# The output projection of a hybrid decoder layer, by one level of Strassen's scheme

## The chip, the cores and the metric

The kernel runs on one core of one Trainium2 chip. The metric is the device time of one execution in microseconds (us); a kernel is run several times and the median counts. TensorE (PE) multiplies matrices, VectorE (DVE), ScalarE (ACT) and GpSimd (POOL) do the element-wise work, SyncE (SP) mostly issues DMAs. A matmul's stationary operand is loaded first (PEld), its moving operand of 512 columns then streams through, and the sums stay in one of eight PSUM banks of 128x512 float32. The working memory is SBUF, with 128 partitions.

## The reference, cut to what matters

```python
h = rmsnorm(x, pre_g)                                # x: (1024, 1024) float32
z = h @ w_in                                         # one input projection, split into the parts below
a_out = chunked_sgu(gelu(a_u), gelu(a_v), ...) * silu(a_gate)    # branch A: (1024, 1024)
b_out = rmsnorm_per_head(gla_chunked(q, k, v, log_a)) * silu(b_gate)   # branch B: (1024, 1024)
mixed = concatenate([a_out, b_out], -1)              # (1024, 2048)
y = mixed @ w_out                                    # w_out: (2048, 1024)
return x + rmsnorm(y, post_g)
```

Only the last two lines are touched: a product of 1024 x 2048 by 2048 x 1024, a norm over each row of the result, and the residual.

## The kernel before

Every large product is done in three matmuls per pair of tiles (mm3, L105 to L109). A float32 operand is split into a rounded part "hi" and the rest "lo", both of the type float32r: ACT casts hi (L102), DVE subtracts it from the source to get lo (L103), and TensorE adds hi*hi + hi*lo + lo*hi into a PSUM bank. A split of a 128x512 tile is thus one ACT and one DVE instruction; the DVE one reads two operands from SBUF.

The order of work is: the norm of x and its transposed, split form hT (four tiles of tag "q" in pool hp); branch B head by head, whose features end up in four tiles mixB (feature-major, 128 features x 1024 tokens at a time); branch A, whose features end up in place in the tiles vn (read through mixed_a: 128 features x 512 tokens); the output projection. In branch A the last steps are, for the eighth group of channels, a projection out of hT, an ACT activation into u (L587) and a DVE product into vn (L592).

The output projection takes the tokens in two halves. For a half it goes through the 16 feature tiles in four groups of four. For each feature tile it loads the 128 rows of w_out (L620, 512 KB, into three slots "raw" of the pool wts), splits both halves of the columns into granules wh and wl (nine slots each) and splits the feature tile into mm. The B features come first, since the A features are the last to be ready. Eight banks hold the sums of four token tiles by two column halves; every group adds 96 matmuls, so there are 2 x 4 x 96 = 768. In the last group of a half each token tile is finished in turn: ACT squares and sums a bank (L653), DVE multiplies it by post_g (L660), DVE and POOL make the reciprocal root (L95, L98), DVE scales and adds the residual (L662), and SP and ACT issue the stores.

Tiles come from pools; tiles of one tag share a number of slots, and a pool that is opened where another was closed takes over its bytes. The kernel states no order by hand. A planner simulates the program when it is built: of the instructions that are ready in its simulated time it puts the one that comes first in the program on the engine's queue, gives out slots, and derives all waits. On the chip each queue then runs in that fixed order. Loads, casts and subtractions of a later tile can so be queued ahead of the work of an earlier one, as far as slots are free. That is how the first w_out loads come to stand in SP's queue some 70 us before the projection begins: the slots "raw" and the granules are those of the input projections before it, and the first two mm tiles have a place of their own in vnp (the later ones take over the bytes of hT).

Of the kernel before, what the change touches and what calls it, by code (L numbers as in the profile page):

```python
# [8 lines left out]
F32 = mybir.dt.float32  # L9
F32R = mybir.dt.float32r  # L10
# [5 lines left out]
P = 128  # L16
# [17 lines left out]
def hybrid_layer(  # L34
# [28 lines left out]
    hp = ctx.enter_context(tc.tile_pool(name="hp", bufs=1))  # L63
# [41 lines left out]
    def mm3(ps, a, b, start, stop):  # L105
        """ps += a^T b, with a and b given as their two parts"""
        nc.tensor.matmul(ps, a[0], b[0], start=start, stop=False)  # L107
        nc.tensor.matmul(ps, a[0], b[1], start=False, stop=False)  # L108
        nc.tensor.matmul(ps, a[1], b[0], start=False, stop=stop)  # L109

    W = 512
    # the pre norm's gain goes into the rows of w_in: one column of it for each k tile
    gain = const.tile([P, KT], F32, name="gain")

    def split_scaled(hi, lo, src, k):
        """the two parts of src times the gain of k tile k"""
        g = gain[:, k : k + 1]
        nc.scalar.activation(out=hi, in_=src, func=AF.Copy, scale=g)  # L118
        nc.vector.scalar_tensor_tensor(  # L119
            out=lo, in0=src, scalar=g, in1=hi.bitcast(F32), op0=ALU.mult, op1=ALU.subtract  # L120
        )
# [10 lines left out]
    def block_a(cols, before=lambda k2: None):  # L132
        """512 columns of w_in, k tile by k tile: [(hi, lo)] of [P, 512]"""
        got = []
        for k2 in range(KT // 2):
            before(k2)
            raw = wts.tile([P, 2, W], F32, tag="raw", name="raw", bufs=3)
# [12 lines left out]
    def block_b(cols):  # L150
        """two times 128 columns of w_in: [(hi, lo)] by k of [P, 256]"""
        got = []
        for k4 in range(KT // 4):
            raw = wts.tile([P, 4, 256], F32, tag="raw", name="raw", bufs=3)
# [19 lines left out]
    def proj_tok(ts, blk):  # L174
        """[tok, col] = h[tok tile] @ w, for the token tiles ts"""
# [8 lines left out]
    def proj_col(hf, blk, i):  # L184
        """[col, tok] = (h @ w)^T for the 128 columns i of a block and a half of the tokens"""
# [8 lines left out]
    # v and gate of the first head, and the low-rank weights, wait in slots of the mixed features  # L194
# [15 lines left out]
    with tc.tile_pool(name="pre", bufs=2) as pre:  # L210
# [48 lines left out]
        for t in range(NT - 2):  # L259
# [6 lines left out]
            if t == 3:  # L266
                # columns by groups of 32: hi, hi, lo, hi
# [13 lines left out]
    mixB = []  # L281
    with tc.tile_pool(name="gla", bufs=1) as gp:
# [12 lines left out]
        # low-rank weights by groups of 32 rows, to meet lr's parts: hi, lo, hi, hi  # L295
# [14 lines left out]
        # lr by groups of 32 rows: h w_hi twice rounded, h w_lo, and what the rounding left  # L310
# [20 lines left out]
        def gates(hd, hf):  # L331
            """exp of b - b_ref, b_ref - b, b_last - b and b, feature-major"""
# [6 lines left out]
            # 16 * log_a = min(z, 0) - ln(1 + exp(-|z|))  # L339
# [38 lines left out]
        def qk(hd, got):  # L378
            """q and k of a head, with their decays, in tiles of two chunks"""
# [42 lines left out]
        def attend(hd, t, got, v, sg, cur):  # L422
            """output of one tile of two chunks, and the state after it"""
# [179 lines left out]
    def mixed(n, hf):  # L603
        """tile n of the mixed features (B first) for a half of the tokens: [P, 4, P]"""
        if n < 8:
            return mixB[n // 2][:, n % 2, hf * 512 : (hf + 1) * 512].rearrange("p (t c) -> p t c", c=P)
        return mixed_a(n - 8, hf)

# [1 line left out]
    with tc.tile_pool(name="outp", bufs=2) as op:  # L610
        pog = op.tile([P, D], F32, name="pog", bufs=1)
        nc.gpsimd.dma_start(pog, row_bc(post_g, D))
        for hf in range(2):
            acc = []
            for n4 in range(0, 16, 4):
                ws, ms = [], []
                for n in range(n4, n4 + 4):
                    e = (n + 8) % 16
                    raw = wts.tile([P, 2, W], F32, tag="raw", name="raw", bufs=3)
                    nc.sync.dma_start(  # L620
                        raw.rearrange("p a b -> p (a b)"), w_out[e * P : (e + 1) * P, :]
                    )
                    ws.append(weight_granules(2, [P, W]))
                    for j in range(2):
                        split(*ws[-1][j], raw[:, j])
                    i = 16 * hf + n
                    if i == 0:
                        mm = vnp.tile([P, 2, 2, 4, P], F32R, tag="wg", name="mm")
                    elif i % 4 == 2:
                        mm = hp.tile([P, 2, 4, 4, P], F32R, tag="q", name="mm", bufs=4)  # L630
                    i = (i - 2) % 4 if i >= 2 else i
                    ms.append((mm[:, 0, i], mm[:, 1, i]))
                    split(*ms[-1], mixed(n, hf))
                for t in range(4):
                    if n4 == 0:
                        acc.append([bank(), bank()])
                    last = n4 == 12
                    order = [(i, j) for i in range(4) for j in range(2)]
                    if last:
                        order.sort(key=lambda o: o[1])  # L640
# [50 lines left out]
```

## Time and profile before

| | before |
|---|---|
| median of 3 runs | 807.33 us (806.49 to 807.36) |
| profiled execution, span from first to last instruction | 805.6 us |
| what lies around the span in the runs | 0.9 to 1.8 us |
| PE busy | 787.2 us (98%) |
| DVE, ACT, POOL busy | 49%, 42%, 16% |
| output projection, first to last matmul | 624.8 to 799.0 us |

The profile gives one execution with the start and length of every instruction, and what ended each wait. Of the profiled execution the page gives the span alone; its own time stands beside the other runs in the second and third line. Matmuls overlap each other in the records (each shows 389 ns, while a new one starts every 0.227 us), so a sum of durations overstates PE; its pace is read from start times.

### The profile page before, as it was taken

To read this page: it belongs to the slowest core of one execution; us is meant where nothing else is said; L and a number is where in the kernel's file an instruction comes from. 1 tells how busy PE (TensorE), PEld (TensorE's weight loads), DVE (VectorE), ACT (ScalarE), POOL (GpSimd) and SP (SyncE) were. 2 spreads that over 40 slices of the span, in tenths; PEclk is the share of its full clock that TensorE was granted. 3 is DMA by queue.
4 is the path that set the end of the run, shared out by engine and by line. 5 is a ranking of instruction groups with operands and counts; after the bars stand their busy time and mean duration, and the time that the engine had idled before them with its cause. 6 is when DMAs were issued, how large, how long until landed. Compare 5 with 4: busy or idle time off the path is not lost.

```text
span 805.6 us, 10163 instructions
## 1 busy us (share of the span) xinstructions
PE 787.2 (98%) x3865; PEld 656.8 (82%) x3865; DVE 392.8 (49%) x736; ACT 336.8 (42%) x678; POOL 126.7 (16%) x161
## 2 busy tenths in 40 slices
PE   5999999999999999999999999999999999999996
PEld 4888888887888788888888888888888888888885
DVE  4536688337633763342424996233332613663235
ACT  6628567336633763241414315343432512542222
POOL 2341243221222122120001350000000000010001
PEclk9999999999999999999999999999999999999999
DMA  9303101003100310031503011111110333473304
GB/s 285 116 8 111 52 1 54 1 1 111 54 1 1 111 53 1 1 105 52 157 1 105 0 53 53 52 53 53 53 53 8 125 104 104 145 264 115 105 27 156
DMA packets 48913, 58.53 MB, mean 73 GB/s; under 512 B 3864, under 2 KB 38688, under 8 KB 48864
## 3 DMA queue, kind: packets, MB, share of 16 engines
q1 hardware_dynamic: 45488, 49.36, 20.0%
q0 software_dynamic: 2224, 7.47, 3.0%
q10 hardware_dynamic: 1152, 1.05, 0.4%
q8 instruction: 30, 0.49, 0.3%
q14 instruction: 19, 0.16, 0.1%
HBM read 53.68 MB, written 4.19 MB: 72 GB/s over the span
## 4 chain that ended last, share of the span: by engine, by line
PE 93%; ACT 3%; DVE 2%; DMA 1%; issue 1%; POOL 0%; SPq 0%; POOLq 0%; DVEq 0%; ACTq 0%
PE ps L107 29%; PE ps L108 29%; PE ps L109 29%; PE ps L571 2%; PE ps L318 1%; PE ps L464 1%; DMA raw<-in_w_in_dram 1%; PE ps L238 1%; PE ps L413 1%; ACT wh L118 0%; ACT L349 0%; PE ps L403 0%; PE ps L405 0%; ACT L348 0%; DVE b L352 0%
## 5 line engine op out<-in xcount | busy, mean ns | idle before, releaser
L107 PE MATMUL ps<-wh,hT 128*128 128x512 f32 x384 | 152.0, 397 | 2.3 <-ACT hT L102 2.3
L107 PE MATMUL ps<-hT,wh 128*128 128x512 f32 x384 | 150.7, 393 | 0.0
L109 PE MATMUL ps<-wh,hT 128*128 128x512 f32 x384 | 150.7, 393 | 0.0
L108 PE MATMUL ps<-wl,hT 128*128 128x512 f32 x384 | 150.3, 392 | 0.0
L109 PE MATMUL ps<-hT,wl 128*128 128x512 f32 x384 | 149.8, 390 | 0.0
L108 PE MATMUL ps<-hT,wh 128*128 128x512 f32 x384 | 149.6, 390 | 0.0
L108 PE MATMUL ps<-wl,mm 128*128 128x512 f32 x256 | 99.3, 389 | 0.0
L109 PE MATMUL ps<-wh,mm 128*128 128x512 f32 x256 | 99.3, 389 | 0.0
L107 PE MATMUL ps<-wh,mm 128*128 128x512 f32 x256 | 96.2, 389 | 0.0
L119 DVE SCALAR_TENSOR_TENSOR wl<-raw,gain,wh 128x256 fp32r<-128x256 f32 (+1 forms) x144 | 87.1, 654 | 18.2 <-ACT wh L118 18.0
L118 ACT ACTIVATE wh<-raw,gain 128x256 fp32r<-128x256 f32 (+1 forms) x144 | 74.1, 573 | 30.6 <-PE ps L108 14.8
L107 PEld LDWEIGHTS ps<-wh,hT 128*128 128x128 f32 x384 | 72.7, 189 | 17.0 <-ACT hT L102 2.7
L109 PEld LDWEIGHTS ps<-wh,hT 128*128 128x128 f32 x384 | 72.5, 189 | 14.9 <-DVE hT L103 0.5
L109 PEld LDWEIGHTS ps<-hT,wl 128*128 128x128 f32 x384 | 72.1, 188 | 15.0
L103 DVE TENSOR_TENSOR wl<-raw,wh 128x512 fp32r<-128x512 f32 x64 | 42.9, 690 | 84.5 <-ACT wh L102 84.5
L108 PEld LDWEIGHTS ps<-wl,hT 128*128 128x128 f32 x384 | 72.7, 189 | 13.9
L108 PEld LDWEIGHTS ps<-hT,wh 128*128 128x128 f32 x384 | 72.2, 188 | 14.6
L107 PEld LDWEIGHTS ps<-hT,wh 128*128 128x128 f32 x384 | 72.2, 188 | 14.2
L102 ACT CAST wh<-raw 128x512 fp32r<-128x512 f32 x64 | 38.7, 622 | 98.8 <-PE ps L109 74.4
L108 PEld LDWEIGHTS ps<-wl,mm 128*128 128x128 f32 x256 | 48.1, 188 | 10.1
L109 PEld LDWEIGHTS ps<-wh,mm 128*128 128x128 f32 x256 | 48.1, 188 | 9.9
L107 PEld LDWEIGHTS ps<-wh,mm 128*128 128x128 f32 x256 | 48.0, 188 | 9.9
(166 smaller groups left out, 927.8 us busy)
## 6 DMA issues: line engine op xcount, KB each, us to landing
raw<-in_w_in_dram SPq DMA_DIRECT2D x80, 256.0 KB, 3.6
raw<-in_w_out_dram SPq DMA_DIRECT2D x32, 512.0 KB, 4.1
raw<-in_w_in_dram SPq DMA_DIRECT2D x8, 512.0 KB, 3.9
xr<-in_x_dram POOLq DMA_DIRECT2D x8, 512.0 KB, 4.4
xt<-in_x_dram SPq DMA_DIRECT2D x7, 512.0 KB, 5.5
out_dram<-yo SPq DMA_DIRECT2D x8, 256.0 KB, 2.1
out_dram<-yo ACTq DMA_DIRECT2D x8, 128.0 KB, 2.1
out_dram<-yo SPq DMA_DIRECT2D x8, 128.0 KB, 2.4
```

What stands on the lines that cost most here:

```text
L102: nc.scalar.copy(out=hi, in_=src)
L103: (eng or nc.vector).tensor_tensor(out=lo, in0=src, in1=hi.bitcast(F32), op=ALU.subtract)
L107: nc.tensor.matmul(ps, a[0], b[0], start=start, stop=False)
L108: nc.tensor.matmul(ps, a[0], b[1], start=False, stop=False)
L109: nc.tensor.matmul(ps, a[1], b[0], start=False, stop=stop)
L118: nc.scalar.activation(out=hi, in_=src, func=AF.Copy, scale=g)
L119: nc.vector.scalar_tensor_tensor(out=lo, in0=src, scalar=g, in1=hi.bitcast(F32), op0=ALU.mult, op1=ALU.subtract)
L238: nc.tensor.transpose(pt[:, k * P : (k + 1) * P], h[:, kk * P : (kk + 1) * P], ident)
L318: nc.tensor.matmul(pl, w_lr[:, k], part, start=(k == 0 and i == 0), stop=(k == KT - 1 and i == 1),)
L413: nc.tensor.transpose(pt[:, j * P : (j + 1) * P], ks[:, 2 * j : 2 * j + 2].rearrange("p n c -> p (n c)"), ident,)
L464: nc.tensor.transpose(ptv[:, k, i], og[:, i, k * P : (k + 1) * P], ident)
L571: nc.tensor.matmul(pt[:, c], part[:, c], wsT[:, g], start=True, stop=True)
```

## The change

The product is cut into blocks: rows of the result into the two token halves, the 2048 features into B (index 1) and A (index 2), the columns of w_out into two halves. Instead of eight block products there are seven, by the form of Strassen's scheme in which sums are reused: with S1 = A21 + A22, S2 = S1 - A11, S3 = A22 - S2 (which is A11 - A21 with the sign that the scheme wants), S4 = A12 - S2 on the left and T1 = B12 - B11, T2 = B22 - T1, T3 = B22 - B12, T4 = T2 - B21 on the right. A block product is 8 feature tiles x 4 token tiles x 3 = 96 matmuls (128x512).

- The left sums are made by POOL, in place, in the feature tiles (32 instructions of 128x512, two SBUF operands each). The right sums are made by DVE (32 of the same size) from newly loaded tiles of w_out; T1 and then T2 stay in eight tiles "kept". Both are then split by ACT and DVE as before.
- Two sets of four banks, u and v, are used in turns. Products 1, 3, 5 and 7 add up in u, 2 and 4 in v, 6 in a new set. Between products ACT copies the state of a set, or DVE adds it, into the result tiles y in SBUF. A set's copy is followed by a whole product on the other set before it is written again.
- The feature tiles of a product are taken one by one (12 matmuls for a feature tile); only the last product holds four of them and then finishes token tile by token tile.
- w_out is loaded in blocks of 128x512 (256 KB): 72 loads, in place of 32 of 512 KB, into six slots "raw".
- All tiles of the stage but the granules wh and wl lie in a new pool at the right end of SBUF. hT and the old "raw" slots now lie there too, and their pools are closed just before the new one is opened (hps.close()). The left split parts have six slots each.

```diff
     mixp = ctx.enter_context(tc.tile_pool(name="mixp", bufs=1))
-    hp = ctx.enter_context(tc.tile_pool(name="hp", bufs=1))
+    hps = ctx.enter_context(ExitStack())
+    rawp = hps.enter_context(tc.tile_pool(name="rawp", bufs=1, side="right"))
+    hp = hps.enter_context(tc.tile_pool(name="hp", bufs=1, side="right"))
...
-    def mm3(ps, a, b, start, stop):
-        """ps += a^T b, with a and b given as their two parts"""
-        nc.tensor.matmul(ps, a[0], b[0], start=start, stop=False)
-        nc.tensor.matmul(ps, a[0], b[1], start=False, stop=False)
-        nc.tensor.matmul(ps, a[1], b[0], start=False, stop=stop)
+    def mm3(ps, a, b, start, stop, goes_on=False):
+
+        how = {"skip_group_check": True} if goes_on else {}
+        nc.tensor.matmul(ps, a[0], b[0], start=start, stop=False, **how)
+        nc.tensor.matmul(ps, a[0], b[1], start=False, stop=False, **how)
+        nc.tensor.matmul(ps, a[1], b[0], start=False, stop=stop, **how)
...
-            raw = wts.tile([P, 2, W], F32, tag="raw", name="raw", bufs=3)
+            raw = rawp.tile([P, 2, W], F32, tag="raw", name="raw", bufs=3)
...
+    hps.close()
+    def tiles_b(j, hf):
+        return mixB[j // 2][:, j % 2, hf * 512 : (hf + 1) * 512].rearrange("p (t c) -> p t c", c=P)
...
+    with tc.tile_pool(name="outp", bufs=1, side="right") as op:
+        pog = op.tile([P, D], F32, name="pog")
         nc.gpsimd.dma_start(pog, row_bc(post_g, D))
+        a11, a21 = ([tiles_b(j, hf) for j in range(8)] for hf in range(2))
+        a12, a22 = ([mixed_a(j, hf) for j in range(8)] for hf in range(2))
+        kept = [op.tile([P, W], F32, tag="kept", name="kept", bufs=8) for _ in range(8)]
+        ptt = nc.gpsimd.tensor_tensor
+        vtt = nc.vector.tensor_tensor
+
+        def load(j, row, col):
+
+            raw = op.tile([P, W], F32, tag="raw", name="raw", bufs=6)
+            r = (8 + j if row == 0 else j) * P
+            nc.sync.dma_start(raw, w_out[r : r + P, col * W : (col + 1) * W])
+            return raw
+
+        def left(j, what):
+
+            if what == "s1":
+                ptt(out=a21[j], in0=a21[j], in1=a22[j], op=ALU.add)
+                return a21[j]
+            if what == "s2":
+                ptt(out=a11[j], in0=a21[j], in1=a11[j], op=ALU.subtract)
+                return a11[j]
+            if what == "s4":
+                ptt(out=a21[j], in0=a12[j], in1=a11[j], op=ALU.subtract)
+                return a21[j]
+            if what == "s3":
+                ptt(out=a11[j], in0=a22[j], in1=a11[j], op=ALU.subtract)
+                return a11[j]
+            return {"a11": a11, "a12": a12, "a22": a22}[what][j]
+
+        def right(j, what):
+
+            if what == "t1":
+                b11, b12 = load(j, 0, 0), load(j, 0, 1)
+                vtt(out=kept[j], in0=b12, in1=b11, op=ALU.subtract)
+                return kept[j]
+            if what == "t2":
+                vtt(out=kept[j], in0=load(j, 1, 1), in1=kept[j], op=ALU.subtract)
+                return kept[j]
+            if what == "t3":
+                b22, b12 = load(j, 1, 1), load(j, 0, 1)
+                vtt(out=b22, in0=b22, in1=b12, op=ALU.subtract)
+                return b22
+            if what == "-t4":
+                b21 = load(j, 1, 0)
+                vtt(out=b21, in0=b21, in1=kept[j], op=ALU.subtract)
+                return b21
+            return load(j, *{"b11": (0, 0), "b21": (1, 0), "b22": (1, 1)}[what])
+
+        def factors(j, l, r):
+            b = weight_granules(1, [P, W])[0]
+            split(*b, right(j, r))
+            a = tuple(op.tile([P, 4, P], F32R, tag="a" + i, name="a" + i, bufs=6) for i in "hl")
+            split(*a, left(j, l))
+            return a, b
+
+        def product(ps, l, r, first, done=None):
+
+            held = []
+            for j in range(8):
+                a, b = factors(j, l, r)
+                held.append((j, a, b))
+                if done and j in (4, 5, 6):
+                    continue
                 for t in range(4):
+                    for i, a, b in held:
+                        mm3(ps[t], [m[:, t] for m in a], b, first and i == 0, i == 7, not first)
+                    if done and j == 7:
+                        done(t)
+                held = []
+
+        def sum_sq(ss, src):
+            junk = op.tile([P, W], F32, tag="junk", name="junk")
+            nc.scalar.activation(
+                out=junk, in_=src, func=AF.Square, scale=D ** -0.5, accum_out=ss
+            )
+
+        C0, C1 = slice(0, W), slice(W, D)
+        y = [[op.tile([P, D], F32, name=f"y{hf}{t}") for t in range(4)] for hf in range(2)]
+        sums = op.tile([P, 2, 4, 2], F32, name="sums")
+        ss = [[sums[:, hf, t] for t in range(4)] for hf in range(2)]
+
+        def finish(hf, t, pieces):
+            r = slice((4 * hf + t) * P, (4 * hf + t + 1) * P)
+            xr = op.tile([P, D], F32, tag="xr", name="xr", bufs=2)
+            nc.gpsimd.dma_start(xr, x[r, :])
+            rstd = op.tile([P, 1], F32, tag="rstd", name="rstd", bufs=2)
+            rsqrt(rstd, ss[hf][t][:, 0:1], ss[hf][t][:, 1:2])
+            for i, c in enumerate(pieces):
+                nc.vector.scalar_tensor_tensor(
+                    out=y[hf][t][:, c], in0=y[hf][t][:, c], scalar=rstd, in1=xr[:, c],
+                    op0=ALU.mult, op1=ALU.add,
+                )
+                (nc.sync, nc.scalar)[i % 2].dma_start(out[r, c], y[hf][t][:, c])
+
+        u = [bank() for _ in range(4)]
+        product(u, "a11", "b11", True)
+        for t in range(4):
+            nc.scalar.copy(out=y[0][t][:, C0], in_=u[t])
+        v = [bank() for _ in range(4)]
+        product(v, "s1", "t1", True)
+        for t in range(4):
+            nc.scalar.copy(out=y[1][t][:, C1], in_=v[t])
+        product(u, "s2", "t2", False)
+        for t in range(4):
+            nc.scalar.copy(out=y[0][t][:, C1], in_=u[t])
+        product(v, "s4", "b22", False)
+        for t in range(4):
+            vtt(out=y[0][t][:, C1], in0=v[t], in1=y[0][t][:, C1], op=ALU.add)
+            sum_sq(ss[0][t][:, 1:2], y[0][t][:, C1])
+        product(u, "s3", "t3", False)
+        for t in range(4):
+            vtt(out=y[1][t][:, C1], in0=u[t], in1=y[1][t][:, C1], op=ALU.add)
+            sum_sq(ss[1][t][:, 1:2], y[1][t][:, C1])
+            ptt(out=y[1][t][:, C1], in0=y[1][t][:, C1], in1=pog[:, C1], op=ALU.mult)
+        v = [bank() for _ in range(4)]
+        product(v, "a12", "b21", True)
+        for t in range(4):
+            vtt(out=y[0][t][:, C0], in0=v[t], in1=y[0][t][:, C0], op=ALU.add)
+            sum_sq(ss[0][t][:, 0:1], y[0][t][:, C0])
+            ptt(out=y[0][t], in0=y[0][t], in1=pog, op=ALU.mult)
+            finish(0, t, (slice(0, D),))
+
+        def done(t):
+            sum_sq(ss[1][t][:, 0:1], u[t])
+            vtt(out=y[1][t][:, C0], in0=u[t], in1=pog[:, C0], op=ALU.mult)
+            finish(1, t, (C1, slice(0, 256), slice(256, W)))
+
+        product(u, "a22", "-t4", False, done)
```

## Rows read from the trace of the kernel before

**Rows 1.** The page: busy time of each engine, and PE in 40 slices of the span.
```profile
PE 787.2 (98%) x3865; PEld 656.8 (82%) x3865; DVE 392.8 (49%) x736; ACT 336.8 (42%) x678; POOL 126.7 (16%) x161
...
PE   5999999999999999999999999999999999999996
```

**Rows 2.** The page: the chain that ended last, by engine.
```profile
PE 93%; ACT 3%; DVE 2%; DMA 1%; issue 1%; POOL 0%; SPq 0%; POOLq 0%; DVEq 0%; ACTq 0%
```

**Rows 3.** Instructions on tile mm: count, duration min/median/max in ns, first and last start.
```profile
L107 PE MATMUL ps<-wh,mm x256: 389/389/389, 624.8 to 798.2; 128*128 128x512 f32 x128
...
L109 PE MATMUL ps<-wh,mm x256: 388/389/389, 625.2 to 798.6; 128*128 128x512 f32 x128
...
L103 DVE TENSOR_TENSOR mm<-vn,mm x16: 683/685/692, 626.9 to 732.9; 128x512 fp32r<-128x512 f32 x16
```

**Rows 4.** Busy time by engine in stretches of the start and of the output projection.
```profile
core 0: us, PE busy (x) PEld busy (x) DVE busy (x) ACT busy (x) POOL busy (x), PEclk, DMA share, GB/s
...
13.00:15.00 2.00, 2.00 (x6) 1.51 (x6) 1.49 (x4) 1.94 (x5) 0.81 (x2) 1.00 1.00 328
...
660.00:680.00 20.00, 20.00 (x90) 16.57 (x89) 7.64 (x12) 6.76 (x12) 0.00 (x0) 1.00 0.33 105
...
700.00:720.00 20.00, 20.00 (x90) 16.54 (x90) 15.21 (x31) 10.02 (x22) 3.49 (x7) 1.00 0.78 258
```

**Rows 5.** Instructions on tile hT from 600 us on.
```profile
L109 PE MATMUL ps<-hT,wl x35: 389/389/393, 599.6 to 624.6; 128*128 128x512 f32 x35
```

**Rows 6.** Timeline (start, length): ACT and DVE after a projection, DVE subtractions back to back.
```profile
601.73 0.59 ACT L587 ACTIVATE u<-ps 128x512 f32<-128x512 f32 x1
...
602.47 0.69 DVE L592 TENSOR_TENSOR vn<-vn,u 128x512 f32<-128x512 f32 x1
...
623.91 3.09 DVE L103 TENSOR_TENSOR mm<-mixB,mm 128x512 fp32r<-128x512 f32 x5
```

**Rows 7.** Timeline where the pool of the output stage opens.
```profile
631.14 0.68 DVE L592 TENSOR_TENSOR vn<-vn,u 128x512 f32<-128x512 f32 x1
...
632.37 0.63 POOL L612 DMA_DIRECT2D pog<-in_post_norm_g_dram  x1 [150.46 <-issue]
```

**Rows 8.** The loads of w_out: issues, and time from issue to landing.
```profile
L620 SPq DMA_DIRECT2D raw<-in_w_out_dram x32: 327/328/340, 554.2 to 773.9; - x32
...
DMA to landing us min/median/max: 3.1/4.1/7.8
```

**Rows 9.** Timeline of the kernel's start.
```profile
2.12 1.93 SPq L140 DMA_DIRECT2D raw<-in_w_in_dram  x4
...
8.95 1.33 ACT L118 ACTIVATE wh<-raw,gain 128x512 fp32r<-128x512 f32 x2 [3.90 <-DMA raw<-in_w_in_dram]
...
11.39 0.63 PE L108 MATMUL ps<-wl,hT 128*128 128x512 f32 x1
...
14.92 0.47 PE L107 MATMUL ps<-wh,hT 128*128 128x512 f32 x1
```

**Rows 10.** POOL's groups by line: busy, mean ns, idle before.
```profile
L103 POOL TENSOR_TENSOR qsl<-m,qsh 128x512 fp32r<-128x512 f32 x8 | 10.3, 1282 | 31.0 <-ACT qsh L102 31.0
```

**Rows 11.** Lines L562 and L119: durations min/median/max in ns.
```profile
L562 POOL TENSOR_TENSOR vn<-vn,gb x4: 4709/4725/4762, 452.1 to 477.1; 128x2048 f32<-128x2048 f32 x4
...
L119 DVE SCALAR_TENSOR_TENSOR wl<-raw,gain,wh x144: 411/484/4806, 9.7 to 577.2; 128x256 fp32r<-128x256 f32 x96, 128x512 fp32r<-128x512 f32 x48
```

**Rows 12.** Timeline: POOL and DVE at the same time, twice.
```profile
95.69 1.37 POOL L361 TENSOR_TENSOR f<-b 128x512 f32<-128x512 f32 x1 [3.90 <-DVE b L352]
...
96.08 1.53 DVE L357 TENSOR_TENSOR d<-b 128x512 f32<-128x512 f32 x1
...
108.70 1.30 POOL L103 TENSOR_TENSOR scl<-scm,sch 128x512 fp32r<-128x512 f32 x1
...
108.87 0.68 DVE L103 TENSOR_TENSOR kstl<-ps,ksth 128x512 fp32r<-128x512 f32 x1
```

**Rows 13.** Timeline of the end: the last scaling and residual.
```profile
800.79 1.54 DVE L662 SCALAR_TENSOR_TENSOR yo<-yo,rstd,xr 128x512 f32<-128x512 f32 x3
```

More of the change, by code (lines that the diff above doesn't have):

```diff
@@ L153, in block_b @@
         for k4 in range(KT // 4):
-            raw = wts.tile([P, 4, 256], F32, tag="raw", name="raw", bufs=3)
+            raw = rawp.tile([P, 4, 256], F32, tag="raw", name="raw", bufs=3)
             for i, c0 in enumerate(cols):
@@ L601, in hybrid_layer @@
                         gating(g)
[L603 to L611, printed above, removed]
-        nc.gpsimd.dma_start(pog, row_bc(post_g, D))
[L613 to L633, printed above, removed]
-                for t in range(4):
[L635 to L640, printed above, removed]
-                    for i, j in order:
-                        mm3(acc[t][j], [m[:, t] for m in ms[i]], ws[i][j], n4 + i == 0, n4 + i == 15)
-                    if not last:
-                        continue
-                    r = slice((4 * hf + t) * P, (4 * hf + t + 1) * P)
-                    xr = op.tile([P, D], F32, tag="xr", name="xr")
-                    nc.gpsimd.dma_start(xr, x[r, :])
-                    ss = op.tile([P, 2], F32, tag="ss", name="ss")
-                    yo = op.tile([P, D], F32, tag="yo", name="yo")
-                    halves = [slice(j * W, (j + 1) * W) for j in range(2)]
-                    for j, c in enumerate(halves):
-                        junk = op.tile([P, W], F32, tag="junk", name="junk", bufs=1)
-                        nc.scalar.activation(
-                            out=junk, in_=acc[t][j], func=AF.Square, scale=D ** -0.5,
-                            accum_out=ss[:, j : j + 1],
-                        )
-                        if j == 1:
-                            rstd = op.tile([P, 1], F32, tag="rstd", name="rstd")
-                            rsqrt(rstd, ss[:, 0:1], ss[:, 1:2])
-                        nc.vector.tensor_tensor(out=yo[:, c], in0=acc[t][j], in1=pog[:, c], op=ALU.mult)
-                    for i, c in enumerate((slice(0, 512), slice(512, 768), slice(768, D))):
-                        nc.vector.scalar_tensor_tensor(
-                            out=yo[:, c], in0=yo[:, c], scalar=rstd, in1=xr[:, c], op0=ALU.mult, op1=ALU.add
-                        )
-                        (nc.sync, nc.scalar)[i % 2].dma_start(out[r, c], yo[:, c])
```

## The prediction

> **What bounds the kernel now.** I read the page first: PE is busy for 98% of the span and its slices are full from the second to the last but one [rows 1]. The chain that ended last says the same: 93% of it is PE [rows 2]. So matmuls that go away are worth their full pace, as long as the others still find their operands in time. Then the stage itself, by the tiles its matmuls read: the 768 matmuls on mm start from 624.8 to 798.6 us, the last ends 0.39 later, at 799.0 [rows 3]. That is 174.2 us / 768 = 0.227 us each, without a hole: the last matmul on hT starts at 624.6 [rows 5] and the first on mm at 624.8. In this stage the feeders have room: in 20 us DVE is busy for 7.6 to 15.2 us, ACT for 6.8 to 10.0, POOL for 0 to 3.5 [rows 4]. Two things keep the seam at 624.8 closed: loads of w_out issued from 554.2 on [rows 8], and operand slots that were free before the last projection ended.
>
> **The change part by part.**
>
> *Matmuls.* Seven products of 96 are 672, in place of 768: 96 x 0.227 = 21.8 us less. Form and operands stay, so the pace does. What is left is 152.5 us.
>
> *The seam: the new pool.* Its slots "raw" and its left parts take over bytes of hT and of the tiles of branch A. What such a take-over waits for is visible once: the first instruction of the old output pool (the load of pog) was issued at 632.37, 0.55 us after the last product into vn ended (631.14 + 0.68 = 631.82), though POOL had been idle for 150 us [rows 7]. I read this as a pool that opens when all the tiles before it on its bytes are done. Then no w_out load can go out before branch A's last product. The last hT matmul ends at 624.6 + 0.4 = 625.0; then ACT makes u and DVE the product, 602.47 + 0.69 - 601.73 = 1.4 us from the start of the one to the end of the other [rows 6]; with some 0.2 for the hand-overs the pool opens at 626.6. From issue to landing takes 3.1 us at least, 4.1 in the median and 7.8 at most [rows 8]. Here six loads of 256 KB and pog go out at once; at the kernel's start, likewise a burst, the first raw tile was used 8.95 - 2.12 = 6.8 us after its issue [rows 9]. I take 4.5, nearer to the median of the same loads: 631.1. Cast (ACT takes 0.59 for an instruction of this size [rows 6]) and subtraction (0.69 [rows 3]) follow, 1.4 with the hand-overs: PE goes on at 632.5, after 7.5 us without work. The bounds: 4.6 (opening with the last hT matmul, landing in 3.1), 12 (opening at 626.6, landing in 7.8, one POOL instruction ahead), and 0 if the bytes are free earlier, which the row of pog speaks against. Before, this cost nothing, because loads, casts and subtractions stood beside the last projection.
>
> *The ramp.* The only matmuls of this trace that follow a PE nearly idle for long are those of the start: from 11.39 to 14.92 nine of them start 0.44 us apart, twice the later pace [rows 9]. The granted clock reads 1.00 (2.4 GHz) even in that stretch [rows 4], so I take the price from the pace: 3.5 us for 8 intervals where 1.8 would do, 1.7 us. Bounds 0 and 1.7; I take 1.7, the only row of its kind. The Trainium skill ("TensorE: Matmul & The Clock Gate", section "Why this matters for your kernels") states that an idle stretch between bursts sends the clock back to its lower level; by it the 1.7 is due after any such seam, no matter what the start was waiting for. No run here shows that yet.
>
> *Feeding.* A feature tile now occupies PE for 12 x 0.227 = 2.72 us. It costs DVE two subtractions (split of the left and of the right tile), in products 2, 3, 5 and 7 a third for the right sum. Back to back a subtraction takes (3.09 - 0.69) / 4 = 0.60 us [rows 6]: 1.2 or 1.8 us out of 2.72. ACT casts twice, some 1.2 us. POOL adds once in products 2 to 5, 1.28 us [rows 10]. Alone, each engine keeps up, and the slots let the feeders run six tiles ahead. But DVE and POOL don't run side by side here. A DVE product that began at 96.08, while POOL worked from 95.69 to 97.06, ended 0.55 us after POOL, at 97.61; one with a PSUM operand, at 108.87, took its usual 0.68 beside POOL [rows 12]. The longest DVE instruction of line L119 took 4.81 us instead of 0.48, the length of a POOL instruction of 4.73 [rows 11]. So every one of the 32 POOL adds displaces DVE work on two SBUF operands. POOL's adds depend only on features and earlier splits, so they are done greedily in products 1 to 3. There DVE has 16 + 24 + 24 = 64 subtractions. 32 pairs of 1.28 + 0.55 are 58.6 us, the other 32 at 0.60 are 19.2: 77.8 us, from 626.6 to 704.4. PE, restarted at 632.5, wants the last tile of product 3 at 632.5 + 65.4 - 2.7 = 695.2. If all 32 adds come first it waits 9 us; if the eight for S3, which follow the splits of S2, come after, 32 - 8 adds end 10 us earlier and it waits for nothing. I take the middle, 4 us, bounds 0 and 9.
>
> The Trainium skill ("SBUF — State Buffer", section "Who interferes with whom") has the rule that speaks against this change: a VectorE instruction with two SBUF inputs and a GpSimd instruction that reads SBUF lock each other out for the whole instruction. The rows show a little less, 0.55 of 0.69 us after POOL's end. By the rule each pair would be 0.14 us longer, 32 x 0.14 = 4.5 us more on this term.
>
> *Later products.* Product 4 needs no third subtraction (9.6 us of DVE in 21.8), so the lead is rebuilt. Product 5 has 24 subtractions and 4 additions from PSUM, 16.8 us; product 6, 16 and 4 beside POOL's four multiplications, 12 + 5.1. Product 7 has 24, four additions, four POOL multiplications of double width (estimate from 1.28: 2.5 each) and four wide scalings (about 1.5): 33 us, of which 18 subtractions (10.8) can be done in product 6. Cost 0; if order costs a tile, up to 3.
>
> *Seams between products.* A set of banks is copied or added while the other set works for 21.8 us; four ACT copies of 0.6 or four DVE additions of 0.6 fit in that. The price is 0 unless they stand in front of the next product's splits (a rival below).
>
> *Loads.* Products 2 and 5 want 512 KB per 2.72 us, 193 GB/s; the trace has 258 in one stretch [rows 4]. Three such pairs fit the six slots: with the median landing a pair every 1.6 us, with 7.8 every 2.8 us, 0.1 late on 16 tiles. Cost 0, at most 2. SP's 72 issues of 0.33 us [rows 8] are 24 us of 152.
>
> *The end.* After the last matmul the same chain follows as now (805.6 - 799.0 = 6.6 us). Token tiles now follow each other at 2.72 us instead of 5.4, against about 0.6 + 0.2 + 1.54 = 2.4 us of DVE for each [rows 13]: cost 0, at most 1.
>
> *Sum.* -21.8 + 7.5 + 1.7 + 4 = -8.6 us. The span becomes 797.0. What lies around it was 0.9 to 1.8 us in the runs of before; their median is 1.7 above the profiled span, so 798.7 us.
>
> **Rivals.**
> 1. *Seam and lock hidden.* The new slots may fall on bytes that are free earlier, or the planner may find other cover. For: before, loads stood 70 us ahead. Against: the row of pog. 807.3 - 21.8 + 0 to 5 = 785.5 to 790.5 us. Chance 0.14.
> 2. *Gain eaten by the feeders.* POOL's adds all come first (9 us), landings cost 2, the last products 3, the seam 7.5, the ramp 1.7: 23.2 against 21.8, so about 808.7; with one or two of the small terms missing, 803. For: DVE and POOL together have as much locked work until product 3 as PE has time. Against: ACT and DVE were idle half of the stage. Range 803 to 809, chance 0.21.
> 3. *Slower: the queues drain at each product's end.* The copies and additions of a finished product come first in the program. If they stand on ACT's and DVE's queues in front of the next product's casts and subtractions, PE finds nothing at each of six seams until copy (0.6), cast (0.6), subtraction (0.7) and hand-overs (0.3) are through: 2.2 us, and with a POOL sum and a load in the chain up to 8. With the seam and ramp paid (9.2), 12.6 us are left: it decides from 2.1 us per seam. Six seams of 4 us give 807.3 - 21.8 + 9.2 + 24 = 818.7. For: queues run in order. Against: slots allow six tiles ahead, and the planner did put loads and casts ahead at the old seam. Chance 0.18.
>
> **How the numbers follow.** The forecast has 0.47, its own range is 793 to 803 us (the seam 4.6 to 12, the lock 0 to 9, not both at an end). For 8 in 10 I take 788 to 808.5: left out are the lower part of rival 1 and most of rival 3. About 0.2% (1.6 us) is what a measurement here can tell from no change. Faster: forecast 0.47, rival 1 0.14, and 0.08 of rival 2, 0.69. Within 0.2%: 0.08 of rival 2. Slower: 0.05 of rival 2 and rival 3, 0.23.
>
> **What would show it.** Right: 672 matmuls on the left parts, 0.227 us apart; one hole of about 7 us in PE behind the last hT matmul, ended by a w_out load; slow matmuls for some 3.5 us behind it; in products 1 to 3 holes of about 1 us ended by DVE, beside POOL adds; full slices from product 4 on. Wrong: loads of w_out issued before 625 us (rival 1); PE waits in products 5 to 7 (rival 2); a hole at each product's end (rival 3). A hole beyond 12 us at the first seam would also break the sum.

## The result, and the profile after

The changed kernel takes 826.5 us (825.97 to 828.26) against 807.35 (806.49 to 808.09) in the same comparison: 1.0242 of before [1.0227, 1.0256], slower by 2.4%. The profiled execution has a span of 825.0 us, 19.4 more than before.

The page of the kernel after, in the lines that answer to [rows 1] and [rows 2] (busy time; PE and its granted clock in 40 slices; the chain that ended last, by engine):

```profile
PE 786.2 (95%) x3769; PEld 640.2 (78%) x3769; DVE 458.0 (56%) x776; ACT 352.7 (43%) x706; POOL 194.7 (24%) x201
...
PE   6999999999999999999999999999998599999991
...
PEclk9999999999999999999999999999999699999996
...
PE 87%; DMA 3%; ACT 3%; DVE 2%; POOL 2%; issue 1%; SPq 0%; DVEq 0%; ACTq 0%; POOLq 0%
```

PE runs 96 matmuls fewer than in [rows 1], as planned, but its busy time is only 1.0 us less. The slices have a hole in places 31 and 32 and an empty end, and in the chain DMA has grown from 1% to 3% and POOL from 0% to 2%. Three places hold the 19.4 us.

**The pace of all matmuls.** The change does not touch the projections ahead of the output, and yet they take longer. The last matmuls on hT in the kernel after, by tile (count, duration min/median/max in ns, first and last start), the answer to [rows 5]:

```profile
L112 PE MATMUL ps<-hT,wl x48: 392/394/397, 599.6 to 636.1; 128*128 128x512 f32 x48
```

The last one starts 11.5 us later (636.1 against 624.6), and each lasts 394 ns instead of 389. The pace shows in any untouched stretch. Twelve matmuls of the same projection (not the same twelve, as the kernel after is some 8 us late by then), before and then after, in the timeline of PE (start, length); between the two lines shown lie eleven matmuls:

```profile
489.55 0.39 PE L107 MATMUL ps<-hT,wh 128*128 128x512 f32 x1
...
492.27 0.39 PE L107 MATMUL ps<-hT,wh 128*128 128x512 f32 x1
```

```profile
489.81 0.40 PE L110 MATMUL ps<-hT,wh 128*128 128x512 f32 x1
...
492.61 0.40 PE L110 MATMUL ps<-hT,wh 128*128 128x512 f32 x1
```

Twelve matmuls take 2.72 us before and 2.80 after: 0.2267 us each against 0.2333 (means over 20 us). The granted clock is 1.00 in both. In the new stage the pace is 0.2333 as well, so its 672 matmuls cost 672 x 0.0066 = 4.4 us more than the prediction's pace allows: 11.5 + 4.4 = 15.9 us together.

**The seam.** The timeline of the kernel after from the last hT matmul on (start, length, in brackets the idle time before and what ended it):

```profile
636.10 0.39 PE L112 MATMUL ps<-hT,wl 128*128 128x512 f32 x1
...
637.15 0.69 DVE L595 TENSOR_TENSOR vn<-vn,u 128x512 f32<-128x512 f32 x1 [3.83 <-ACT u L590]
637.92 14.38 SPq L627 DMA_DIRECT2D raw<-in_w_out_dram  x9
...
638.58 9.42 DVE L105 TENSOR_TENSOR al<-mixB,ah 128x512 fp32r<-128x512 f32 x6 [0.73 <-ACT ah L104]
...
641.05 0.61 ACT L104 CAST wh<-raw 128x512 fp32r<-128x512 f32 x1
641.12 9.68 POOL L636 TENSOR_TENSOR mixB<-mixB 128x512 f32<-128x512 f32 x6
...
641.72 2.08 PE L110 MATMUL ps<-wh,ah 128*128 128x512 f32 x4 [5.23 <-ACT wh L104]
...
647.92 4.64 DVE L105 TENSOR_TENSOR wl<-raw,wh 128x512 fp32r<-128x512 f32 x4
...
649.72 0.79 PE L111 MATMUL ps<-wl,ah 128*128 128x512 f32 x1 [5.92 <-DVE wl L105]
...
650.31 0.63 PE L112 MATMUL ps<-wh,al 128*128 128x512 f32 x1
650.73 0.63 PE L111 MATMUL ps<-wl,ah 128*128 128x512 f32 x1
```

The pool opens when the last product into vn ends, and the first w_out load is issued 0.08 us later. PE gets the first hi part after 5.2 us, does four matmuls and waits 5.9 us more for the lo part. On DVE's queue six left subtractions stand in front of that lo part, and they take 1.57 us each (9.42 / 6), while POOL makes left sums at 1.61 each (9.68 / 6): against 0.60 [rows 6] and 1.28 [rows 10]. Where both have work without a break, from 642.4 to 649.1, each of the two engines starts one every 1.68 us. After the wait the matmuls start 0.43 us apart until 653.3. The windows of this stretch (busy time and count of PE, PEld, DVE, ACT, POOL; then the granted clock, the DMA share and GB/s), the answer to [rows 4]:

```profile
640.00:650.00 10.00, 2.36 (x5) 1.45 (x6) 10.00 (x8) 4.76 (x9) 9.98 (x9) 0.50 0.82 285
650.00:660.00 10.00, 10.00 (x37) 7.95 (x38) 9.97 (x12) 3.77 (x7) 4.03 (x3) 0.84 0.70 224
```

The clock stands at 0.50, the lower of its levels (1.2 GHz), after PE has been nearly idle from 636.5 on, and comes back in the next window. From the end of the last hT matmul (636.5) to that of the last of the stage (807.4) are 170.9 us; 672 x 0.2333 = 156.8 of them are matmuls at pace, so seam and ramp cost 14.1. No other wait of PE shows in the stage.

**The tail.** The last 17.6 us hold no matmul (before: 6.6). The chain of waits there (start, length, what), which [rows 13] ended with three scalings in a row:

```profile
799.54 5.59 DMA xr<-in_x_dram
...
805.22 1.29 DVE y L705
...
806.80 5.61 DMA xr<-in_x_dram
...
812.50 1.55 DVE y L705 x3
...
814.34 5.29 DMA xr<-in_x_dram
...
819.73 0.75 DVE y L705
```

Loads of the residual and scalings take turns: xr has two slots, and a load of 512 KB waits until a scaling has freed one. Six of the eight loads are issued only after 797 us. The scalings that had to free the slots for them stood behind POOL's four wide multiplications by post_g for the first token half, which the same chain has from 784.9 to 796.9. Sum of the three places: 11.5 + 4.4 - 21.8 + 14.1 + 11.0 = 19.2 of 19.4 us.

### The profile page after: what moved, and what is told of

Same layout as the page of the kernel before. It is cut to its first block, busy times and chain, and to the rows that moved or that the text cites. A ratio compares the mean times of both kernels' runs of the same rounds, so it can differ in the third digit from the quotient of the medians.

```text
span 825.0 us, 10259 instructions
## 1 busy us (share of the span) xinstructions
PE 786.2 (95%) x3769; PEld 640.2 (78%) x3769; DVE 458.0 (56%) x776; ACT 352.7 (43%) x706; POOL 194.7 (24%) x201
## 4 chain that ended last, share of the span: by engine, by line
PE 87%; DMA 3%; ACT 3%; DVE 2%; POOL 2%; issue 1%; SPq 0%; DVEq 0%; ACTq 0%; POOLq 0%
PE ps L111 27%; PE ps L112 27%; PE ps L110 27%; DMA xr<-in_x_dram 2%; PE ps L574 2%; POOL y L736 1%; PE ps L321 1%; DMA raw<-in_w_out_dram 1%; PE ps L467 1%; PE ps L241 1%; DMA raw<-in_w_in_dram 1%; PE ps L416 0%; DVE y L705 0%; ACT wh L121 0%; ACT L352 0%
## 5 line engine op out<-in xcount | busy, mean ns | idle before, releaser
L110 PE MATMUL ps<-wh,hT 128*128 128x512 f32 x384 | 154.2, 402 | 1.9 <-ACT hT L104 1.9
L110 PE MATMUL ps<-hT,wh 128*128 128x512 f32 x384 | 152.8, 398 | 0.0
L112 PE MATMUL ps<-wh,hT 128*128 128x512 f32 x384 | 152.5, 398 | 0.0
L111 PE MATMUL ps<-hT,wh 128*128 128x512 f32 x384 | 151.7, 395 | 0.0
L111 PE MATMUL ps<-wl,ah 128*128 128x512 f32 x224 | 89.6, 400 | 5.9 <-DVE wl L105 5.9
L110 PE MATMUL ps<-wh,ah 128*128 128x512 f32 x224 | 88.5, 400 | 5.2 <-ACT wh L104 5.2
L112 PE MATMUL ps<-wh,al 128*128 128x512 f32 x224 | 89.4, 399 | 0.0
L110 PEld LDWEIGHTS ps<-hT,wh 128*128 128x128 f32 x384 | 72.1, 188 | 16.4
L590 ACT ACTIVATE u<-ps 128x512 f32<-128x512 f32 x32 | 19.0, 594 | 101.3 <-PE ps L112 101.2
L575 DVE TENSOR_TENSOR vn<-ps,bs 128x512 f32<-128x512 f32 x16 | 11.0, 686 | 88.7 <-PE ps L574 88.7
L111 PEld LDWEIGHTS ps<-wl,ah 128*128 128x128 f32 x224 | 42.5, 190 | 17.1 <-DVE wl L105 6.6
L110 PEld LDWEIGHTS ps<-wh,ah 128*128 128x128 f32 x224 | 42.5, 190 | 16.0 <-ACT wh L104 5.7
L112 PEld LDWEIGHTS ps<-wh,al 128*128 128x128 f32 x224 | 42.6, 190 | 10.4
```

The source lines that it names most:

```text
L110: nc.tensor.matmul(ps, a[0], b[0], start=start, stop=False, **how)
L111: nc.tensor.matmul(ps, a[0], b[1], start=False, stop=False, **how)
L112: nc.tensor.matmul(ps, a[1], b[0], start=False, stop=stop, **how)
L575: nc.vector.tensor_tensor(out=part, in0=pt, in1=bs[:, g : g + 1].to_broadcast([P, 4, P]), op=ALU.add)
L590: nc.scalar.activation(out=u, in_=pu.rearrange("p (c t) -> p c t", c=4), func=func)
```

## The experiments

What the changed kernel (after) and the eleven experiments gave; "last" is the end of the last matmul, the pace that of the late projections and of the output stage:

| kernel | median us | ratio to before, 95% | span | last, tail | pace hT, stage |
|---|---|---|---|---|---|
| after | 826.5 | 1.0242 [1.0227, 1.0256] | 825.0 | 807.4, 17.6 | 0.2333, 0.2333 |
| e1_pad_right | 814.2 | 1.0074 [1.0050, 1.0099] | 811.2 | 793.4, 17.8 | 0.2267, 0.2289 |
| e2_before_pad | 824.1 | 1.0204 [1.0180, 1.0227] | 821.8 | 815.3, 6.5 | 0.2333, 0.2333 |
| e3_xr | 821.5 | 1.0170 [1.0145, 1.0194] | 822.1 | 812.0, 10.1 | 0.2333, 0.2333 |
| e4_pad_xr | 810.1 | 1.0030 [1.0013, 1.0046] | 806.3 | 796.1, 10.2 | 0.2267, 0.2289 |
| e5_left_dve | 799.9 | 0.9901 [0.9878, 0.9924] | 798.3 | 788.9, 9.4 | 0.2267, 0.2289 |
| e6_pad96 | 818.3 | 1.0130 [1.0106, 1.0155] | 815.9 | 805.9, 10.0 | 0.2333, 0.2324 |
| e7_before_all32 | 807.5 | 0.9996 [0.9987, 1.0005] | 805.1 | 798.5, 6.6 | 0.2267, 0.2267 |
| e8_no_pool | 800.5 | 0.9913 [0.9883, 0.9942] | 797.5 | 789.0, 8.5 | 0.2267, 0.2289 |
| e9_pad_parts | 797.2 | 0.9872 [0.9857, 0.9888] | 796.3 | 787.8, 8.5 | 0.2267, 0.2267 |
| e10_early | 788.2 | 0.9762 [0.9745, 0.9779] | 786.6 | 778.1, 8.5 | 0.2267, 0.2267 |
| e11_before_pad64 | 821.8 | 1.0180 [1.0162, 1.0198] | 819.1 | 812.5, 6.6 | 0.2290, 0.2333 |

**Is it the place of the operands?** In the built programs hT begins at byte 100032 of a partition before and at 151520 after. The weight granules begin at 30400 before and at 18112 after, and all of them and the tiles of hT are a multiple of 256 bytes long. So the distance from the granules to hT is 69632 bytes before, a multiple of 256, and 133408 after, which is 32 more than one. Two kernels put 32 bytes in, one to take the effect away from the changed kernel, one to give it to the kernel before, whose work stays as it was.

e1, in the kernel after, the first pool at the right end:

```diff
+    padp = ctx.enter_context(tc.tile_pool(name="padp", bufs=1, side="right"))
+    pad = padp.tile([P, 8], F32, name="pad")
+    nc.vector.memset(pad, 0.0)
     hps = ctx.enter_context(ExitStack())
```

> The changed kernel with a 32-byte tile allocated first at the right end, so that every tile there starts 32 bytes lower: hT at byte 151488 instead of 151520 of each partition, a multiple of 64 like the tiles on the left. Theory A (TensorE's pace hangs on whether both operands start at a multiple of 64 bytes): matmuls 0.227 us apart instead of 0.233 all through, 3072 - 96 = 2976 of them of 512 columns x 0.0065 = 19 us less, about 807 us. Theory B (the pace hangs on the side or the distance from the weights, or on the waits of this program): pace stays 0.233, 826 us.

The last matmuls on hT in e1, to be read against the same line of the kernel after (392/394/397, up to 636.1):

```profile
L115 PE MATMUL ps<-hT,wl x34: 388/389/393, 599.9 to 624.1; 128*128 128x512 f32 x34
```

e2, in the kernel before:

```diff
+    padp = ctx.enter_context(tc.tile_pool(name="padp", bufs=1))
+    pad = padp.tile([P, 8], F32, name="pad")
+    nc.vector.memset(pad, 0.0)
     hp = ctx.enter_context(tc.tile_pool(name="hp", bufs=1))
```

> The kernel before, nothing else changed, with a 32-byte tile allocated in front of hT, so that hT, mm and all tiles behind them start at 32 modulo 64 while the weight granules stay at 0. Theory A: pace 0.233 us wherever hT or mm is an operand, 3072 x 0.0065 = 20 us more, 827 us. Theory B: pace 0.227, 807 us.

The tile mm in e2, to be read against [rows 3]:

```profile
L110 PE MATMUL ps<-wh,mm x256: 395/395/397, 635.9 to 814.4; 128*128 128x512 f32 x128
```

The stage of e2 begins 11.1 us later than in [rows 3] (635.9 against 624.8) and ends 16.3 later (last start 814.9 against 798.6). Thirty-two unused bytes make the kernel before 16.3 us slower (824.1 against 807.8), with no instruction of its work changed. In e1 the late projections are back at 0.2267 and their last matmul starts at 624.1, while seam (waits of 5.2 and 5.9) and tail stay. So the place is the cause of the pace; of the 13.8 us by which the span falls, 12.0 lie ahead of the stage.

Both sizes were missed: e2 was to cost 20 us and cost 16.3, e1 was to gain 19 and gained 12.3. In e2 the delay grows by 7.1 us from 360 us to the stage, about as the pace says, but only by some 5 before that, where the matmuls on hT stand between branch B's smaller ones and the pace alone would make 8; why is not shown. And the output stage of e1 runs at 0.2289, a pace that neither theory had.

**Is it the residual's two slots?** e3 takes the residual tiles into slots of the B features, which are free by then, so that all eight have a place; e4 does that and the pad of e1:

```diff
+        xrs = []
...
-            xr = op.tile([P, D], F32, tag="xr", name="xr", bufs=2)
+            i = 4 * hf + t
+            if i % 2 == 0:
+                xrs.append(slot_b([P, 2, D]))
+            xr = xrs[-1][:, i % 2]
```

> The changed kernel, with the rows of x for the residual loaded into the four slots of the B features (free after product 5) instead of two slots of their own: eight loads early, none waits for a scaling. If the end (17.6 us from the last matmul's end) is late because each 5.5 us load of x waits for a slot, it shrinks to some 7 to 8 us: 816 us. Rival: the end is late because POOL's multiplications and DVE's scalings lock each other out; then it stays above 14 us: 823 us or more.

> Both edits, the 32-byte tile at the right end and the residual rows in the slots of the B features. If both causes are right and independent: 826.5 - 19 - 10 = 797 us, which is near the sum that was predicted without them (798.7). If either is wrong, 807 to 826.

The tail falls from 17.6 to 10.1 us and no load stands in its chain any more, but e3 gains only 5.0 us. The chain of e3 a little earlier, and the one new wait of PE in product 7 (us in total, times, longest):

```profile
790.65 5.24 POOL y L741 x2
795.89 0.99 POOL rstd L100
796.88 5.64 POOL y L741 x2
```

```profile
PE ps L112 <- DVE al L105: 3.0, 1, 3.0
```

POOL's wide multiplications by post_g, 2.6 to 2.8 us each, came next, beside DVE work with two SBUF operands, and PE now waited 3.0 us for a left part; in the profiled execution, the slowest of e3's four, the last matmul ends 4.6 us later than in the kernel after, 1.2 of them from ahead of the stage, where nothing was changed. In e4 the gains of e1 and e3 add up (12.3 and 5.0 by themselves, 16.4 together), but the 797 us expected were missed by 13: that sum took 19 and 10 for the two edits. What is left in e4 are PE's two waits at the seam, still 5.2 and 5.9, one of 2.4 in product 7, and a tail of 10.2 where the kernel before has 6.6.

**Is it DVE and POOL at the seam?** e5 is e4 with all four left sums, S1 to S4, on DVE:

```diff
-                ptt(out=a21[j], in0=a21[j], in1=a22[j], op=ALU.add)
+                vtt(out=a21[j], in0=a21[j], in1=a22[j], op=ALU.add)
...
-                ptt(out=a11[j], in0=a21[j], in1=a11[j], op=ALU.subtract)
+                vtt(out=a11[j], in0=a21[j], in1=a11[j], op=ALU.subtract)
...
```

> e4_pad_xr with the 32 left sums made by DVE instead of POOL. In e4 the hole behind the last hT matmul is 13 us, though the first w_out load has landed long before: six subtractions of left parts stand in front of the first one of a right part on DVE's queue and take 9.4 us beside POOL's sums, where six back to back take 3.7. Theory (POOL and DVE lock each other out): they take 3.7 us, the hole shrinks by about 5 us, 805 us. Rival (the hole is the loads' landing and the queue's order, DVE with 32 more instructions only gets later): same or slower, 810 us or more.

The seam of e5 in the timeline (between the lines shown, DVE makes three left sums of 0.69):

```profile
627.58 1.30 DVE L108 TENSOR_TENSOR al<-mixB,ah 128x512 fp32r<-128x512 f32 x2
...
630.59 1.29 DVE L108 TENSOR_TENSOR al<-mixB,ah 128x512 fp32r<-128x512 f32 x2
630.71 2.08 PE L113 MATMUL ps<-wh,ah 128*128 128x512 f32 x4 [5.23 <-ACT wh L107]
...
633.00 1.29 DVE L108 TENSOR_TENSOR wl<-raw,wh 128x512 fp32r<-128x512 f32 x2
633.74 0.79 PE L114 MATMUL ps<-wl,ah 128*128 128x512 f32 x1 [0.95 <-DVE wl L108]
```

DVE does the sums as well and is still through earlier: two subtractions in 1.30 us instead of 1.57 for one. The wait for the first lo part falls from 5.9 to 1.0, the 2.4 in product 7 are gone, and the span falls by 8.0 (of which 4.9 + 2.4 by these waits). The kernel is now 1.0% faster than before. The Trainium skill ("SBUF — State Buffer", section "Who interferes with whom") says that a VectorE instruction with two SBUF inputs and a GpSimd instruction that reads SBUF exclude each other for the whole instruction. The trace of the kernel after agrees that the two engines take turns, with one instruction of each per 1.68 us, a little less than the 0.60 + 1.28 = 1.88 of strict turns; in e5 a DVE instruction takes 0.65.

e8 is e5 with the multiplications by post_g on DVE too (two lines from ptt to vtt).

> e5_left_dve with the multiplications by post_g on DVE as well: nothing of size is left on POOL in the stage. In e4 PE had some 6 us of holes near 785 to 795 us, where subtractions of the last product stood behind scalings that waited for POOL. By the lock theory these go and the end is that of the kernel before (6.6 us behind the last matmul): 797 to 800 us. Rival (DVE, at some 133 of 152 us, becomes the bound): 805 us or more.

Of the 6 us of holes that the expectation counts in e4, the trace shows one of 2.4, and e5 had already taken that away. The tail becomes 8.5 instead of 9.4, not the 6.6 expected, and the medians (800.5 and 799.9) don't tell e8 from e5. Inconclusive as a gain; it stays in the next kernels.

**What of the place counts?** Three kernels asked for the rule: e6 is e4 with 96 bytes instead of 32; e7 puts 32 bytes in front of the pool wts of the kernel before, so that granules and hT move together; e11 puts 64 bytes in front of hT in the kernel before.

```diff
-    pad = padp.tile([P, 8], F32, name="pad")
+    pad = padp.tile([P, 24], F32, name="pad")   # e6;  e11: [P, 16] in e2
```

> e4_pad_xr with 96 bytes instead of 32 at the right end: every tile there 64 bytes lower, so hT at 0 modulo 128 (in e4: 64) and the left parts ah, al at 64 (in e4: 0); the weight granules are at 64. In e4 the pace is 0.2267 us with hT and 0.2289 with ah, al. Theory (a smaller step hangs on the address modulo 128): the two change places, 0.2289 in the input projections (2304 x 0.0022 = 5 us more) and 0.2267 in the output stage (1.5 us less), 814 us. Rival (the output stage is slower for another reason, such as DVE's or the DMAs' traffic): both stay, 810 us.

> The kernel before with the 32-byte tile in front of the weight granules, so that both operands of every matmul of 512 columns start at 32 modulo 64. If each operand's own start counts: 0.233 us or slower, 824 us or more. If only the distance of the two modulo 64 counts: 0.2267, 807 us.

> The kernel before with a 64-byte tile in front of hT, so that hT and mm start 64 bytes beyond a distance of a multiple of 256 from the weights. If only the start modulo 64 or the distance modulo 64 counts: pace 0.2267, 807 us. If the distance modulo 256 and its sign count, as in the traces so far (moving minus stationary operand 0: 0.2267; 64: 0.2289; 128: 0.2325; 192 or odd multiples of 32: 0.233): with hT moving (q, k, u and gate projections) 64, 0.2289; with hT or mm stationary (v and gate by token, output) 192, 0.233; about 1300 x 0.0022 + 1770 x 0.0065 = 14 us more, 821 us.

Tile mm in e7 and then in e11:

```profile
L110 PE MATMUL ps<-wh,mm x256: 389/389/389, 624.2 to 797.6; 128*128 128x512 f32 x128
```

```profile
L110 PE MATMUL ps<-wh,mm x256: 393/393/398, 633.1 to 811.6; 128*128 128x512 f32 x128
```

e7 is the kernel before to 0.1%: a start of each operand that is no multiple of 64 costs nothing if both are shifted alike (here by 32 bytes). That ended the first wording of the theory. e6 missed too (818.3 where 814 was expected): its hT is slow as the moving operand (0.2333) and nearly normal as the stationary one (0.2289). What fits all runs is the distance of the two starts, moving minus stationary, modulo 256 bytes. e11 was predicted from that and came within 1 us of it (821.8 for 821), with hT at 0.2290 where it moves, and the features, which stand, at 0.2333.

| distance, modulo 256 | where | us per matmul |
|---|---|---|
| 0 | before; e7; hT in e1, e4, e5, e8; all late work in e9, e10 | 0.2267 |
| 64 | left parts in e1, e4, e5, e8; hT stationary in e6; hT moving in e11 | 0.2289 to 0.2290 |
| 128 | left parts in e6 | 0.2324 |
| 192 | hT moving in e6; hT stationary and features in e11 | 0.2333 |
| 32 and 224 | after, e2, e3 | 0.2333 |

**The rest of the gain.** e9 is e8 with 192 bytes behind the left parts, so that these too lie at distance 0. e10 is e9 and puts the first four w_out tiles of product 1 into a slot of vnp that is free long before, with the first two left parts in granules:

```diff
         product(u, "a11", "b11", True)
+        padq = op.tile([P, 48], F32, name="padq")    # e9
...
+        early = vnp.tile([P, 4, W], F32, tag="wg", name="early")    # e10
...
+            if r == "b11" and j < 4:
+                nc.sync.dma_start(early[:, j], w_out[(8 + j) * P : (9 + j) * P, 0:W])
+                split(*b, early[:, j])
...
+            if r == "b11" and j < 2:
+                a = weight_granules(1, [P, 4, P])[0]
+                split(*a, left(j, l))
```

> e8_no_pool with a 192-byte tile behind the left parts, so that ah and al start 192 bytes lower: their distance to the weight granules becomes a multiple of 256 bytes like hT's (in e8 it is 192 modulo 256). Theory (the pace hangs on the distance of the two operands modulo 256 bytes): 0.2267 instead of 0.2289 us in the output stage, 672 x 0.0022 = 1.5 us less, 799 us, seen in the trace rather than in the time. Rival (the output stage has its own pace for another reason): 0.2289 stays.

> e9_pad_parts with cover for the first seam: the first four w_out tiles of product 1 go into the slot of branch A's norm weights (free since its last norm), and the first two left parts into weight granules. So loads and splits of the first tiles can stand beside the last projection of branch A. In e8 the hole there is 8.2 us and some 2 us of slow matmuls follow it. Theory (the pool's take-over alone makes the hole): both go, 9 to 10 us less, 790 us. Rival (the planner puts them late all the same, or the next tiles are late instead): 796 us or more.

In e9 the stage runs at 0.2267, as the theory said, and the span falls by 1.2 us (797.5 to 796.3), near the 1.5 expected. The medians fall by 3.3 (800.5 to 797.2), but e8's runs alone lie between 798.0 and 804.3.

The page of e10 (busy time; PE and its granted clock in 40 slices), and its PE timeline at the seam:

```profile
PE 766.1 (97%) x3769; PEld 639.2 (81%) x3769; DVE 445.6 (57%) x818; ACT 352.0 (45%) x706; POOL 127.7 (16%) x161
...
PE   5999999999999999999999999999999999999995
...
PEclk9999999999999999999999999999999999999998
```

```profile
625.35 0.39 PE L115 MATMUL ps<-hT,wl 128*128 128x512 f32 x1
625.58 0.39 PE L113 MATMUL ps<-wh 128*128 128x512 f32 x1
625.81 0.39 PE L114 MATMUL ps<-wl,wh 128*128 128x512 f32 x1
...
777.67 0.39 PE L115 MATMUL ps<-wh,al 128*128 128x512 f32 x1
```

The first matmul of the stage follows the last one on hT after 0.23 us, the granted clock reads 1.00 all through the stage, and the trace shows no wait of PE in the stage: 625.6 to 778.1, 152.5 us, the stage that the prediction had worked out before its losses. At 788.2 us e10 beats both kernels.

## Why the prediction was wrong

The span was forecast at 797.0 and came to 825.0. Of these 28.0 us, 15.9 are the pace, 11.0 the tail (all of it, as the forecast put nothing there) and 14.1 - 13.2 = 0.9 the seam; the rest is rounding.

- **Failed: "Form and operands stay, so the pace does."** The form stays; the operands move. The diff puts pool hp at the right end, and I priced that line only for the bytes that it frees, not for where it lays hT and the left parts. Their distance to the granules went from 0 to 32 or 224 modulo 256, and each matmul from 0.2267 to 0.2333 us, in the projections too, of which the prediction says nothing. e2 shows this cost by itself (16.3 us). No row of before could have priced it, since hT and the features lie at distance 0 there; but the line was in the diff, and it should have stood as an unknown with bounds.
- **Failed: "The end", "cost 0, at most 1".** I held DVE's 2.4 us against the 2.72 us of a token tile and left out the residual: two slots, loads of 5.3 to 5.6 us, each behind the scaling that frees its slot. Before, token tiles came every 5.4 us and the loads were ahead. It cost 11.0; in e3 7.5 of them go with the slots, though only 5.0 reach the median, as POOL's and DVE's work for the last tiles is late next.
- **Right in sum, in part by luck: seam, ramp and lock.** 14.1 us stand against 13.2, but the terms miss in opposite directions. The pool opened as read from the row of pog, 1.4 us after the last hT matmul; the load landed faster than I took (the first cast is 3.1 us behind the first issue), and PE began on the hi parts alone, so the hole up to the first matmul was 5.2 us and not 7.5. The ramp is 3.6 us for eight intervals against 1.9, so 1.7, as forecast. Behind the hole the granted clock read 0.50, the row that the prediction lacked. By the Trainium skill ("TensorE: Matmul & The Clock Gate", section "Why this matters for your kernels") an idle stretch between bursts sends the clock back to its lower level; the trace agrees. The lock between DVE and POOL cost 4.9 us where 4 were forecast (a wait of 5.9, of which 1.0 is left in e5), but at once, in front of the first lo part; I had spread it over products 1 to 3, where no other wait showed. Of the rest, 1.0 is that wait and 1.1 the four matmuls between the two waits, which took 2.08 us at the lower clock.
- **Right: the number of matmuls** (96 fewer), no wait at the seams between products (rival 3's holes are not there), no late load of w_out, and no wait of PE in products 5 to 7 (rival 2).
- **Not this kernel's, but e10's time: rival 1.** Here seam and lock were not hidden. In e10, where edits take away pace, seam and lock and most of the tail, the time is 788.2, inside the 785.5 to 790.5 of rival 1. So nothing was wrong with the count of seven products; the losses came with what moved beside them.

## What to carry to other kernels

When a change moves a pool, compare the pace of matmuls that it does not touch, before anything else, and work out the distance between the starts of the moving and the stationary tiles: here 32 unused bytes cost the kernel before 2.0% and gave back 1.5% of the kernel after. When a stage gets faster, hold every double-buffered load of its last tiles against the new interval, not only the engines' work. And put loads that open a stage where they need not wait for the stage before, since a hole costs its length and then the ramp.

## What the hardware showed unexpectedly

In these kernels TensorE's pace for float32r matmuls of 512 columns depends on the distance between its two operands in SBUF, the start of the moving one minus that of the stationary one, modulo 256 bytes: 0.2267 us at 0, 0.2289 at 64, 0.2324 at 128, 0.2333 at 192, 32 and 224, with the granted clock at 1.00 throughout. That the start of one operand by itself does not count is shown by e7, for 32 bytes. Why the distance counts, and why 64 and 192 differ, stays open; distances of 96 and 160, other column counts and other types were not tried.
